# Attention outputs kept in DRAM until the merge, three more projections by seven products, and the merge's pools one block earlier

## The chip, the cores and the metric

The kernel runs on one core of a Trainium2 chip. The metric is the device time of one execution in microseconds (us). TensorE (PE) multiplies matrices, VectorE (DVE) and ScalarE (ACT) do elementwise work, GpSimd (POOL) and SyncE (SP) mostly issue transfers.

## The reference, cut to what matters

One decoder layer on 256 tokens of width 2048, in fp32, with 256 memory tokens:

```python
h = rmsnorm(x, attn_norm)
gq, gk, gv, gr, ga1, sq, sk, sv, mq, gates = split(h @ w_in)
log_a = log_sigmoid(ga1 @ gla_w_a2 + gla_b_a) / 16
o_gla = rmsnorm(gla_mixer(gq, gk, gv, log_a))              # 4 heads, d_k 128, d_v 256
y_gla = (o_gla * silu(gr)) @ w_br_gla
y_sb  = stick_breaking_mixer(rmsnorm(sq), rmsnorm(sk), sv) @ w_br_sb     # 8 heads of 128
m_k, m_v = split(rmsnorm(mem, mem_norm) @ w_mem_kv)
y_mem = memory_mixer(rmsnorm(mq), rmsnorm(m_k), m_v) @ w_br_mem          # 4 heads of 256
g = sigmoid(gates)
x = x + (g[0] * y_gla + g[1] * y_sb + g[2] * y_mem) @ w_o
gate, up = split(rmsnorm(x, ffn_norm) @ w_gate_up)          # width 5632 each
x = x + (silu(gate) * up) @ w_down
```

## The kernel before

Every product of fp32 matrices is made of three matmuls on rounded halves: high by high, high by low, low by high. The activations lie transposed as such pairs (`xTh`/`xTl`; `oh`/`ol` for attention outputs). Weights come from DRAM in tiles of 1 MB (`raw`, four k-tiles of 128x512), loaded by SP into slots of the list `free_raw`. Each half of a raw tile is split when it is needed: ACT casts it to the high part (`wh`, L137), DVE subtracts to get the low part (`wl`, L138). The two go into a split pair, which `parts()` takes in turn from the pools in `splits`. A pair feeds 128x512 matmuls into accumulators (`acc`, `tmp`) in PSUM.

`gemm` makes one block of 512 output columns, 12 matmuls for a pair (L209 to L211). `sgemm` makes two blocks at once. Over the first `2p` k-tiles it uses seven products instead of eight (`p1` to `p7`, L248 to L251, 6 matmuls for a pair), and over the rest plain products (`rest`, 12 for a pair). Its weight operands are sums of raw tiles, made by DVE (L263) or by POOL's accumulating loads (L305, L325); its activation operands (`forms`: `sh`, `sl`) are made once by `make_forms`. `put` sends a finished product on: a copy on ACT (L288) into an accumulator or a spare tile, or a subtraction on DVE (L290). `p5` is copied to a spare (L319). `result` adds the spare to the accumulator (L380). The list `seq` sets the order of products and rests.

Side work (norms with `normed_T`, attention, transposes) is written as generators in `background`; `step()` runs one piece after each pair, `flush()` runs what is left. A scheduler then sets each engine's order; an engine works in its order, and a wait holds up all that stands behind it.

The order of the program: `mems` and the memory projections `mk` and `mv` (about 100 us), evacuated from PSUM by ACT (L473); `mq` by `gemm`; `sq`, `sk`, `sv_` by `sgemm` with memory attention and norms beside them; `gqk` and `gv` by `gemm` with stick-breaking attention beside them; the decay projection `w_ga` (L762 to L764); `gr` by `gemm`, with the linear attention `gla()` begun behind its first block; four blocks of the first gate (`O_G`) with `w_br_mem`, merged by DVE (L936); release of the attention pools, making of `ring2` and `mrg`; two passes of `w_gate` by `sgemm` with `w_br_sb` and `w_br_gla`; `w_o`; the feed-forward network in three parts.

Pools share room. `opool` holds the pairs of the memory tokens, then of the outputs `o_mem` and `o_sb`, then of `o_gla`. The sigmoid of `gr` and of the first gate takes three ACT operations and one on DVE (L775 to L778), and `gr` is scaled at L907. Transposes are at L431 and their scaled split at L140 and L141.

Of the kernel before, what the change touches and what calls it, by code (L numbers as in the profile page):

```python
# [77 lines left out]
def trunk(ctx: ExitStack, tc: tile.TileContext, a, out):  # L78
# [137 lines left out]
    def sgemm(xs, forms, w, blks, p, row0=0, late=False, moved=False):  # L216
# [517 lines left out]
    def s_out(h):  # L734
# [34 lines left out]
    def sigmoid(dst, o, t, table):  # L769


        if table:
            act.activation(dst, o, AF.Sigmoid, scale=r_x[:, t : t + 1])
        else:
            act.activation(dst, o, AF.Exp, scale=nr_x[:, t : t + 1])  # L775
            dve.tensor_scalar(dst, dst, 3e38, None, op0=ALU.min)
            act.activation(dst, dst, AF.Ln, bias=1.0)
            act.activation(dst, dst, AF.Exp, scale=-1.0)  # L778
# [8 lines left out]
    gr = section("gr", "b")  # L787

    def gla():
        for t in range(2):  # L790
# [55 lines left out]
            og = opool.tile([P, GH, GDV], F32, name="g_og", tag="g_og")  # L846
# [276 lines left out]
```

## Time and profile before

| what | value |
|---|---|
| median of three runs | 1645.92 us (1645.72 to 1649.11) |
| profiled execution, its own time | 1647.21 us |
| its span in the trace | 1645.4 us |
| mean granted clock of TensorE | 0.999 |
| read from HBM, written to it | 320.89 MB, 8.39 MB |

The span runs from the first to the last instruction; an execution's own time has a little more around it. "Granted clock" is the share of TensorE's full speed that it was given; 1.00 is full speed.

### The profile page before, as it was taken

To read this page: it belongs to the slowest core of one execution; us is meant where nothing else is said; L and a number is where in the kernel's file an instruction comes from. 1 tells how busy PE (TensorE), PEld (TensorE's weight loads), DVE (VectorE), ACT (ScalarE), POOL (GpSimd) and SP (SyncE) were. 2 spreads that over 40 slices of the span, in tenths; PEclk is the share of its full clock that TensorE was granted. 3 is DMA by queue.
4 is the path that set the end of the run, shared out by engine and by line. 5 is a ranking of instruction groups with operands and counts; after the bars stand their busy time and mean duration, and the time that the engine had idled before them with its cause. 6 is when DMAs were issued, how large, how long until landed. Compare 5 with 4: busy or idle time off the path is not lost.

```text
span 1645.4 us, 19330 instructions
## 1 busy us (share of the span) xinstructions
PE 1629.8 (99%) x7314; PEld 1334.9 (81%) x7314; DVE 1291.2 (78%) x1491; ACT 988.0 (60%) x1204; POOL 53.8 (3%) x70
## 2 busy tenths in 40 slices
PE   8999999999999999999999999999999999999998
PEld 6888787888877878888888888888888888888887
DVE  6857788764565667887897798988888998888994
ACT  7755666654644556556555666666666666666662
POOL 0000000000000000000000000000110000110000
PEclk9999999999999999999999999999999999999999
DMA  8784575544544467667556758686897686897692
GB/s 327 280 325 125 189 249 158 200 161 156 183 154 154 157 228 284 191 215 255 174 210 220 254 181 259 216 298 234 258 274 255 193 302 240 257 271 253 193 343 89
DMA packets 59406, 368.82 MB, mean 224 GB/s; under 512 B 6544, under 2 KB 11152, under 8 KB 16688
## 3 DMA queue, kind: packets, MB, share of 16 engines
q1 hardware_dynamic: 49968, 320.17, 53.4%
q0 software_dynamic: 8704, 46.67, 14.2%
q8 instruction: 57, 0.93, 0.2%
q10 hardware_dynamic: 640, 0.75, 0.1%
q14 instruction: 37, 0.30, 0.1%
HBM read 320.89 MB, written 8.39 MB: 200 GB/s over the span
## 4 chain that ended last, share of the span: by engine, by line
PE 96%; DVE 1%; DMA 1%; ACT 1%; issue 0%; ACTq 0%; DVEq 0%
PE acc L250 15%; PE acc L251 15%; PE acc L248 15%; PE acc L209 10%; PE acc L210 10%; PE acc L211 10%; PE tmp L250 5%; PE tmp L251 5%; PE tmp L248 5%; PE tmp L431 2%; DVE wl L138 1%; ACT wh L137 1%; DMA raw<-in_w_gate_up 1%; DMA raw<-in_w_mem_kv 0%; PE tmp L635 0%; PE tmp L863 0%
## 5 line engine op out<-in xcount | busy, mean ns | idle before, releaser
L138 DVE TENSOR_TENSOR wl<-raw,wh 128x1024 fp32r<-128x1024 f32 (+1 forms) x728 | 876.9, 1220 | 278.4 <-ACT wh L137 267.4
L137 ACT CAST wh<-raw 128x1024 fp32r<-128x1024 f32 (+1 forms) x728 | 753.9, 1051 | 536.1 <-PE acc L211 212.9
L251 PE MATMUL acc<-wh,hl 128*128 128x512 f32 x452 | 175.9, 389 | 0.0
L250 PE MATMUL acc<-wl,hh 128*128 128x512 f32 x452 | 175.9, 389 | 0.0
L248 PE MATMUL acc<-wh,hh 128*128 128x512 f32 x452 | 175.8, 390 | 0.0
L209 PE MATMUL acc<-wh,xTh 128*128 128x512 f32 x384 | 152.7, 398 | 0.0
L211 PE MATMUL acc<-wh,xTl 128*128 128x512 f32 x384 | 149.9, 390 | 0.0
L210 PE MATMUL acc<-wl,xTh 128*128 128x512 f32 x384 | 149.8, 390 | 0.0
L263 DVE TENSOR_TENSOR raw<-raw 128x1024 f32<-128x1024 f32 x115 | 139.7, 1221 | 4.5 <-DMA raw<-in_w_gate_up 3.0
L209 PE MATMUL acc<-wh,oh 128*128 128x512 f32 x320 | 125.2, 393 | 2.6 <-ACT wh L137 1.6
L210 PE MATMUL acc<-wl,oh 128*128 128x512 f32 x320 | 124.9, 390 | 1.1 <-DVE wl L138 1.1
L211 PE MATMUL acc<-wh,ol 128*128 128x512 f32 x320 | 124.8, 390 | 0.0
L248 PE MATMUL acc<-wh,xTh 128*128 128x512 f32 x280 | 110.1, 395 | 1.3 <-ACT wh L137 1.3
L250 PE MATMUL acc<-wl,xTh 128*128 128x512 f32 x280 | 109.7, 392 | 0.5 <-DVE wl L138 0.5
L251 PE MATMUL acc<-wh,xTl 128*128 128x512 f32 x280 | 109.4, 391 | 0.0
L250 PEld LDWEIGHTS acc<-wl,hh 128*128 128x128 f32 x452 | 84.9, 188 | 17.7
L248 PEld LDWEIGHTS acc<-wh,hh 128*128 128x128 f32 x452 | 84.7, 188 | 17.8 <-ACT wh L137 0.2
L251 PEld LDWEIGHTS acc<-wh,hl 128*128 128x128 f32 x452 | 84.8, 188 | 17.6
L248 PE MATMUL tmp<-wh,sh 128*128 128x512 f32 x222 | 89.4, 403 | 1.8 <-ACT wh L137 1.7
L250 PE MATMUL tmp<-wl,sh 128*128 128x512 f32 x222 | 87.3, 393 | 0.7 <-DVE wl L138 0.7
L251 PE MATMUL tmp<-wh,sl 128*128 128x512 f32 x222 | 87.6, 395 | 0.0
L209 PEld LDWEIGHTS acc<-wh,xTh 128*128 128x128 f32 x384 | 72.2, 188 | 16.4 <-issue 2.2
(297 smaller groups left out, 2497.1 us busy)
## 6 DMA issues: line engine op xcount, KB each, us to landing
raw<-in_w_gate_up SPq DMA_DIRECT2D x88, 1024.0 KB, 5.9
raw<-in_w_in SPq DMA_DIRECT2D x72, 1024.0 KB, 4.9
raw<-in_w_down SPq DMA_DIRECT2D x44, 1024.0 KB, 6.5
raw<-raw POOLq DMA_DIRECT2D x35, 1024.0 KB, 7.9
raw<-in_w_gate SPq DMA_DIRECT2D x32, 1024.0 KB, 4.9
raw<-in_w_o SPq DMA_DIRECT2D x16, 1024.0 KB, 5.0
raw<-in_w_mem_kv SPq DMA_DIRECT2D x15, 1024.0 KB, 5.4
raw<-in_w_br_mem SPq DMA_DIRECT2D x8, 1024.0 KB, 5.2
```

Source lines behind the costliest of these rows:

```text
L137: act.copy(hi, src)
L138: dve.tensor_tensor(lo, src, hi.bitcast(F32), op=ALU.subtract)
L209: pe.matmul(o[t][:], xh[:, s], wh[:, j], start=k == 0, stop=False)
L210: pe.matmul(o[t][:], xh[:, s], wl[:, j], start=False, stop=False)
L211: pe.matmul(o[t][:], xl[:, s], wh[:, j], start=False, stop=k == nk - 1)
L248: pe.matmul(dst[:], xh, wh, start=id(dst) not in begun, stop=False, skip_group_check=True)
L250: pe.matmul(dst[:], xh, wl, start=False, stop=False, skip_group_check=True)
L251: pe.matmul(dst[:], xl, wh, start=False, stop=last, skip_group_check=True)
L263: dve.tensor_tensor(x, x, y, op=ALU.add)
L431: pe.transpose(dst, src, ident)
```

## The change

Memory attention's and stick-breaking attention's outputs no longer stay in SBUF as split pairs. `put_out` copies each piece (ACT, L639) and writes it to DRAM (`od_mem`, `od_sb`); `fetch_out` loads each back with one transfer of 1 MB behind `gr` and splits it there. In the room that `opool` held until then lies `ring_a`, two raw slots and two split pairs; the memory tokens' pairs lie in the same room before it, in a pool `mems`. `gqk`, `gv` go through `sgemm` with `p` = 2 and `gr` with `p` = 4, and `gr` stands ahead of `w_ga`. `ring2` and `mrg` are made ahead of the last `O_G` block. `seq` has one form for all calls that are not `late`, and the POOL sum in `p2` becomes the default (`w_down` keeps DVE's).

```diff
             prod(o[0, 0], single(0, 0), 11, last)
-            if moved:
+            if moved and not late:
                 nc.gpsimd.dma_start(q[11][0][:, :p], q[21][0][:, :p], accum_op=ALU.add)
...
         def q4(last):
-            prod(o[1, 0], single(0, 1), 11, last, *([] if moved else [(11, 21)]))
+            prod(o[1, 0], single(0, 1), 11, last, *([] if moved and not late else [(11, 21)]))
         def p5():
...
             seq = [a, *l21, b, *l11, *r0, *r1[:1], (made,), g, *l22, *r1[1:2], h, e, *l12, *r1[2:3], i, f, *r1[3:]]
-        elif moved:
-            seq = [a, g, *r0[:2], h, *r0[2:], b, e, *r1[:2], i, *r1[2:3], f, *r1[3:]]
-        elif p == SP:
-            seq = [a, g, *r0[:2], h, *r0[2:], e, *r1[:2], i, b, *r1[2:3], f, *r1[3:]]
         else:
-            seq = [a, *l21, g, *r0[:2], h, *r0[2:], e, *l12, *r1[:1], i, *l22, b, *l11, *r1[1:3], f, *r1[3:]]
+            seq = [a, *l21, *r0[:2], g, *r0[2:], h, *l22, b, *l11, e, *l12, *r1[:2], i, *r1[2:3], f, *r1[3:]]
         uses = {21: [a, g, h, f, *l21], 22: [g, h, i, *l22], 11: [b, f, *l11], 12: [h, e, *l12]}
...
     g_gla = gain["gla_out_norm"]
-    opool = tc.alloc_tile_pool(name="opool", bufs=2)
+    opool = tc.alloc_tile_pool(name="mems", bufs=2, side="right", reuse_waits="tile")
     sec = tc.alloc_tile_pool(name="sec", bufs=1)
...
     def outT():
-        return [opool.tile([P, 8, T], F32R, tag=f"o{x}", name=f"o{x}") for x in "hl"]
+        return [opool.tile([P, 8, T], F32R, tag="o", name=f"o{x}", bufs=4) for x in "hl"]
     mems = load_T([outT(), outT()], a["memT"], g_mem, mempool)
...
     att = tc.alloc_tile_pool(name="att", bufs=2)
-    pre = tc.alloc_tile_pool(name="pre", bufs=1, reuse_waits="tile")
-    free_raw.extend([(pre, "raw", 1), (opool, "oh", 2), (opool, "ol", 2)])
+    pre = widen("pre", 1, 0, "left")
+    opool.release()
+    ring_a = widen("ring_a", 2, 2)
     def ring(tag, bufs, dtype=F32):
...
         return ring("rd", 2, F32R)
-    o_mem = outT()
+    def outside(name):
+        return dram.tile([P, 8, T], F32, name=name)
+    def put_out(o, c, src):
+        n = src.shape[1] // T
+        v = rb()[:, : n * T]
+        act.copy(v, src)
+        nc.scalar.dma_start(o[:, c : c + n], v.rearrange("p (c t) -> p c t", c=n))
+    def fetch_out(o):
+        high, low = outT()
+        def work():
+            raw, done = loads()
+            v = raw[:].rearrange("p g n -> p (g n)").rearrange("p (c t) -> p c t", c=8)
+            nc.sync.dma_start(v, o[:])
+            yield
+            for c in range(0, 8, 4):
+                split(high[:, c : c + 4], low[:, c : c + 4], v[:, c : c + 4])
+                if c == 4:
+                    done()
+                yield
+        background.append(work())
+        return high, low
+    od_mem, od_sb = outside("od_mem"), outside("od_sb")
     m_pr, m_prT = {}, {}
...
                 )
-        split(*(x[:, 2 * h : 2 * h + 2].rearrange("p c t -> p (c t)") for x in o_mem), o[:])
-    def wide(dst, c0):
-        for j, result in sgemm(xs, sx, w_in, (c0 // NB, c0 // NB + 1), SP, moved=True):
+        put_out(od_mem, 2 * h, o[:])
+    def wide(dst, c0, p=SP):
+        for j, result in sgemm(xs, sx, w_in, (c0 // NB, c0 // NB + 1), p):
             for t in range(2):
...
-    o_sb = outT()
+    def sigmoid(dst, o, t, table):
+        if table:
+            act.activation(dst, o, AF.Sigmoid, scale=r_x[:, t : t + 1])
...
         pe.matmul(o[:, P:T], sv_[:, 1, h * SD : (h + 1) * SD], ls[:, T:W], start=False, stop=True)
-        split(o_sb[0][:, h], o_sb[1][:, h], o[:, :T])
+        put_out(od_sb, h, o[:, :T])
     flush()
...
     gqk, gv = section("gqk", "a"), section("gv", "d")
-    project(gqk, xs, w_in, O_GQ, r_x)
-    project(gv, xs, w_in, O_GV, r_x)
-    free_raw[:] = [x for x in free_raw if x[0] is not pre]
-    pre.release()
+    wide(gqk, O_GQ, 2)
+    wide(gv, O_GV, 2)
+    flush()
+    sqT = None
+    gr = section("gr", "b")
+    for j, result in sgemm(xs, sx, w_in, (O_GR // NB, O_GR // NB + 1), SP):
+        for t in range(2):
+            sg, o = ra()[:], result(t)
+            sigmoid(sg, o, t, False)
+            v = gr[:, t, j * NB : (j + 1) * NB]
+            act.activation(v, o, AF.Copy, scale=r_x[:, t : t + 1])
+            dve.tensor_tensor(v, v, sg, op=ALU.mult)
+    narrow(ring_a)
+    opool = tc.alloc_tile_pool(name="opool", bufs=4, side="right", reuse_waits="tile")
+    o_mem, o_sb = fetch_out(od_mem), fetch_out(od_sb)
+    narrow(pre)
     gl = tc.alloc_tile_pool(name="gl", bufs=1, reuse_waits="tile")
...
                     yield
-    for n in range(0, MIX, NB):
-        o = gemm(xs, w_in, O_GR + n)
-        if n == 0:
-            background.append(gla())
-        for t in range(2):
-            sg = gate()
-            sigmoid(sg, o[t][:], t, False)
-            v = gr[:, t, n : n + NB]
-            act.activation(v, o[t][:], AF.Copy, scale=r_x[:, t : t + 1])
-            dve.tensor_tensor(v, v, sg, op=ALU.mult)
+    background.append(gla())
     def to_chunks(src, n, hi, lo, gain):
...
     for n in range(0, D, NB):
+        if n + NB == D:
+            flush()
+            gl.release()
+            att.release()
+            sec.release()
+            ring2 = widen("ring2", 3, 1, "left")
+            kit = mrg = tc.alloc_tile_pool(name="mrg", bufs=1, reuse_waits="tile")
         g = gemm(xs, w_in, O_G + n)
...
         merge(sg, gemm(xo, a["w_br_mem"], n), n, True)
-    flush()
-    gl.release()
-    att.release()
-    sec.release()
-    widen("ring2", 3, 1)
-    kit = mrg = tc.alloc_tile_pool(name="mrg", bufs=1, reuse_waits="tile")
     background.append(gla_T())
...
             blks = (n0 // NB, n0 // NB + 1)
-            for j, result in sgemm(fs, sd, a["w_down"], blks, 4, row0=4 * part[0]):
+            for j, result in sgemm(fs, sd, a["w_down"], blks, 4, row0=4 * part[0], moved=False):
                 n = n0 + j * NB
...
```

The three places below show orders of instructions with the numbers of the tiles; nothing in them is a time. In the changed kernel most lines have moved by 4 to 8 and more: L145 and L146 are the cast and the subtraction of `split` (before: L137, L138), L271 is DVE's sum (L263), L298 and L384 the subtraction in `put` and the addition in `result` (L290, L380), L477 the evacuation of `mk`, `mv`, `mq` (L473), L736 to L739 the sigmoid (L775 to L778), L796 the scaling of `gr` (L907), L913 the square in `gla` (L872).

**First place: DVE at the start of the call for `sv_`.** `raw_2112` (before) and `raw_2123` (after) are its first raw tile, L487 is the norm of `sk`. Before:

```order
L263 TENSOR_TENSOR raw_2112<-raw_2112,raw_2148 128x1024
L380 TENSOR_TENSOR two_2043<-acc_1735,two_2043 128x512
L138 TENSOR_TENSOR wl_2132<-raw_2112,wh_2131 128x1024
L138 TENSOR_TENSOR wl_2152<-raw_2112,wh_2151 128x1024
L380 TENSOR_TENSOR two_2043<-acc_1736,two_2043 128x512
L487 TENSOR_REDUCE hn_ss_2124<-ra_2128 128x4
L487 TENSOR_REDUCE hn_ss_2124<-ra_2141 128x4
L263 TENSOR_TENSOR raw_2112<-raw_2112,raw_2148 128x1024
L487 TENSOR_REDUCE hn_ss_2124<-ra_2144 128x4
L263 TENSOR_TENSOR raw_2112<-raw_2112,raw_2242 128x1024
L146 TENSOR_SCALAR rs_m_2161<-hn_ss_2124 128x16
L138 TENSOR_TENSOR wl_2190<-raw_2112,wh_2189 128x1024
```

Of the change:

```order
L146 TENSOR_TENSOR wl_2126<-raw_2123,wh_2125 128x1024
L298 TENSOR_TENSOR two_2054<-two_1656,tmp_1748 128x512
L271 TENSOR_TENSOR raw_2123<-raw_2123,raw_2221 128x1024
L146 TENSOR_TENSOR wl_2143<-raw_2123,wh_2142 128x1024
L146 TENSOR_TENSOR wl_2162<-raw_2159,wh_2161 128x1024
L271 TENSOR_TENSOR raw_2123<-raw_2123,raw_2221 128x1024
L384 TENSOR_TENSOR two_2054<-acc_1746,two_2054 128x512
L146 TENSOR_TENSOR wl_2205<-raw_2159,wh_2204 128x1024
L146 TENSOR_TENSOR wl_2225<-raw_2123,wh_2224 128x1024
```

Ahead of the second L271 sum there are now the subtractions of `wl_2143` and `wl_2162`, the latter for the first rest, and the reductions of the norm no longer stand between the two sums.

**Second place: ACT from `gr` over `w_ga` to the first `O_G` block.** Before, `w_ga` (`wh_3275`, `wh_3303`) stands behind `gv`, and the first block of `gr` (`wh_3342`) follows:

```order
L137 CAST wh_3234<-raw_3232 128x1024
L137 CAST wh_3250<-raw_3232 128x1024
L137 CAST wh_3275<-raw_3272 128x1024
L137 CAST wh_3303<-raw_3272 128x1024
L137 CAST wh_3342<-raw_3340 128x1024
L473 ACTIVATE gv_2483<-acc_3128,r_x_114 128x512
L473 ACTIVATE gv_2483<-acc_3129,r_x_114 128x512
L137 CAST wh_3358<-raw_3340 128x1024
```

Of the change, where `wh_3674` and `wh_3702` are `w_ga`'s, `oh_3663` and `oh_3665` the fetched outputs, `two_3572` a finished product of `gr`, and `wh_3753` the first of `O_G`:

```order
L145 CAST wh_3674<-raw_3671 128x1024
L296 COPY two_3572<-tmp_3331 128x512
L145 CAST wh_3702<-raw_3671 128x1024
L145 CAST oh_3663<-raw_3732 128x1024 x2
L145 CAST oh_3665<-raw_3738 128x1024 x2
L736 ACTIVATE ra_3620<-two_3572,nr_x_118 128x512
L796 ACTIVATE gr_3326<-two_3572,r_x_117 128x512
L736 ACTIVATE ra_3644<-acc_3328,nr_x_118 128x512
L738 ACTIVATE ra_3620<-ra_3620 128x512
L796 ACTIVATE gr_3326<-acc_3328,r_x_117 128x512
L739 ACTIVATE ra_3620<-ra_3620 128x512
L738 ACTIVATE ra_3644<-ra_3644 128x512
```

Four casts of fetched outputs and the sigmoids of `gr` now stand between `w_ga`'s casts and the first cast of `O_G`.

**Third place: ACT at the start of the last `O_G` block.** Before, this is the end of the last block, where `wh_4763` is `w_br_mem`'s last and `wh_4815` the first of `w_gate`:

```order
L775 ACTIVATE sg_4699<-acc_4561,nr_x_115 128x512
L777 ACTIVATE sg_4699<-sg_4699 128x512
L775 ACTIVATE sg_4700<-acc_4562,nr_x_115 128x512
L778 ACTIVATE sg_4699<-sg_4699 128x512
L137 CAST wh_4763<-raw_4745 128x1024
L777 ACTIVATE sg_4700<-sg_4700 128x512
L137 CAST wh_4815<-raw_4796 128x1024
L778 ACTIVATE sg_4700<-sg_4700 128x512
L137 CAST wh_4798<-raw_4796 128x1024
```

Of the change, where `wh_4649` is `w_br_mem`'s last of the third block, `wh_4680` and `wh_4696` the first two of the last block, and `wh_4680` lies in `ring2`:

```order
L736 ACTIVATE sg_4584<-acc_4364,nr_x_118 128x512
L145 CAST wh_4649<-raw_4631 128x1024
L738 ACTIVATE sg_4584<-sg_4584 128x512
L145 CAST wh_4696<-raw_4678 128x1024
L739 ACTIVATE sg_4584<-sg_4584 128x512
L145 CAST wh_4714<-raw_4712 128x1024
L145 CAST wh_4730<-raw_4712 128x1024
L145 CAST wh_4748<-raw_4746 128x1024
L145 CAST wh_4680<-raw_4678 128x1024
L145 CAST wh_4764<-raw_4746 128x1024
```

The half that the block uses first is now cast behind four others of the block, `wh_4748` the last of them.

## Rows read from the trace of the kernel before

**Rows 1.** The page's first part: busy time, share of the span and instructions of each engine.

```profile
PE 1629.8 (99%) x7314; PEld 1334.9 (81%) x7314; DVE 1291.2 (78%) x1491; ACT 988.0 (60%) x1204; POOL 53.8 (3%) x70
```

**Rows 2.** Windows: PE, PEld, DVE, ACT, POOL busy (x starts), clock, DMA share, GB/s.

```profile
178.00:182.00 4.00, 2.60 (x11) 1.54 (x10) 2.41 (x5) 3.98 (x8) 0.00 (x0) 1.00 0.00 0
249.00:257.00 8.00, 6.36 (x20) 4.27 (x19) 8.00 (x14) 5.39 (x7) 0.85 (x1) 0.79 0.68 131
...
604.00:615.00 11.00, 8.38 (x38) 5.78 (x37) 9.54 (x13) 7.38 (x11) 0.86 (x1) 1.00 0.82 263
```

**Rows 3.** PE's timeline at place A; start, duration, what, idle before it.

```profile
179.57 0.73 PE L248 MATMUL acc<-wh,xTh 128*128 128x512 f32 x2 [0.87 <-ACT wh L137]
180.84 0.50 PE L250 MATMUL acc<-wl,xTh 128*128 128x512 f32 x1 [0.53 <-DVE wl L138]
```

**Rows 4.** PE's timeline at place B, the start of the call for `sv_`.

```profile
251.45 0.50 PE L248 MATMUL tmp<-wh,sh 128*128 128x512 f32 x1 [1.01 <-ACT wh L137]
252.39 0.73 PE L248 MATMUL acc<-wh,xTh 128*128 128x512 f32 x2 [0.45 <-ACT wh L137]
253.31 0.80 PE L250 MATMUL tmp<-wl,sh 128*128 128x512 f32 x1 [0.18 <-DVE wl L138]
```

**Rows 5.** DVE's timeline at place B.

```profile
249.10 1.22 DVE L263 TENSOR_TENSOR raw<-raw 128x1024 f32<-128x1024 f32 x1
...
252.03 1.22 DVE L138 TENSOR_TENSOR wl<-raw,wh 128x1024 fp32r<-128x1024 f32 x1
```

**Rows 6.** PE's and ACT's timelines at place C.

```profile
606.79 0.50 PE L250 MATMUL tmp<-wl,xTh 128*128 128x512 f32 x1 [1.32 <-DVE wl L138]
...
609.19 0.39 PE L251 MATMUL tmp<-wh,xTl 128*128 128x512 f32 x1
610.30 0.50 PE L248 MATMUL tmp<-wh,sh 128*128 128x512 f32 x1 [0.73 <-ACT wh L137]
...
611.76 0.50 PE L250 MATMUL tmp<-wl,sh 128*128 128x512 f32 x1 [0.51 <-DVE wl L138]
...
605.29 0.84 ACT L140 ACTIVATE oh<-tmp,vecs 128x256 fp32r<-128x256 f32 x2 [5.76 <-PE tmp L431]
608.25 2.00 ACT L137 CAST wh<-raw 128x1024 fp32r<-128x1024 f32 x2 [2.13 <-PE tmp L251]
```

**Rows 7.** ACT's timeline from the end of `mv` into `mq`.

```profile
98.74 0.69 ACT L473 ACTIVATE mv_mqT<-acc,r_mem 128x512 f32<-128x512 f32 x1 [0.57 <-PE acc L211]
99.33 1.04 ACT L137 CAST wh<-raw 128x1024 fp32r<-128x1024 f32 x1
101.46 1.05 ACT L137 CAST wh<-raw 128x1024 fp32r<-128x1024 f32 x1 [1.09 <-PE acc L211]
104.18 1.05 ACT L137 CAST wh<-raw 128x1024 fp32r<-128x1024 f32 x1 [1.67 <-PE acc L211]
```

**Rows 8.** Groups of ACT and DVE: count, busy us, mean ns, idle before.

```profile
L137 ACT CAST wh<-raw 128x1024 fp32r<-128x1024 f32 x726 | 752.7, 1052 | 534.9 <-PE acc L211 212.9 <-PE acc L251 197.0 <-DVE raw L263 52.4
...
L288 ACT COPY acc<-tmp 128x512 f32<-128x512 f32 x23 | 13.2, 572 | 16.0 <-PE tmp L251 15.7
...
L138 DVE TENSOR_TENSOR wl<-raw,wh 128x1024 fp32r<-128x1024 f32 x726 | 875.5, 1222 | 278.4 <-ACT wh L137 267.4
```

**Rows 9.** ACT's timeline behind the second block of `gr`.

```profile
422.42 0.69 ACT L775 ACTIVATE sg<-acc,nr_x 128x512 f32<-128x512 f32 x1 [0.31 <-PE acc L211]
...
426.45 1.04 ACT L137 CAST wh<-raw 128x1024 fp32r<-128x1024 f32 x1
```

**Rows 10.** PE's timeline in `w_ga`, its first two of 48 matmuls.

```profile
396.04 0.28 PE L762 MATMUL tmp<-xTh,wh 128*128 128x256 f32 x1
396.15 0.28 PE L763 MATMUL tmp<-xTl,wh 128*128 128x256 f32 x1
```

**Rows 11.** DMA issues: count, KB each, us from issue to landing.

```profile
raw<-in_w_in SPq DMA_DIRECT2D x72, 1024.0 KB, 4.9
...
raw<-raw POOLq DMA_DIRECT2D x35, 1024.0 KB, 7.9
```

More of the change, by code (lines that the diff above doesn't have):

```diff
@@ L88, in trunk, with widen, narrow @@
     free_raw, splits, turn = [], [], [0]
-    def widen(name, raw, w):
-        pool = ctx.enter_context(tc.tile_pool(name=name, bufs=1, side="right", reuse_waits="tile"))
-        free_raw.extend([(pool, "raw", raw)] * raw)
+    def widen(name, raw, w, side="right"):
+        pool = tc.alloc_tile_pool(name=name, bufs=1, side=side, reuse_waits="tile")
+        free_raw.extend([(pool, raw)] * raw)
         splits.extend([(pool, w)] * w)
-    pad = ctx.enter_context(tc.tile_pool(name="pad", bufs=1, side="right"))
+        return pool
+    def narrow(pool):
+        for x in (free_raw, splits):
+            x[:] = [y for y in x if y[0] is not pool]
+        pool.release()
+    pad = tc.alloc_tile_pool(name="pad", bufs=1, side="right")
     pad.tile([P, PAD], F32, name="pad")
-    widen("ring1", 3, 4)
+    ring1 = widen("ring1", 3, 4)
+    gog = tc.alloc_tile_pool(name="gog", bufs=2, side="right")
     small = ctx.enter_context(tc.tile_pool(name="small", bufs=2))
@@ L161, in loads @@
     def loads():
-        slot = pool, tag, bufs = free_raw.pop(0)
-        return pool.tile([P, KG, NB], F32, tag=tag, name="raw", bufs=bufs), lambda: free_raw.append(slot)
+        slot = pool, bufs = free_raw.pop(0)
+        return pool.tile([P, KG, NB], F32, tag="raw", name="raw", bufs=bufs), lambda: free_raw.append(slot)
     def parts():
@@ L178, in piece @@
         if not halves:
-            two = opool.tile([P, 2, NB], F32, name="two", tag="g_og")
+            two = gog.tile([P, 2, NB], F32, name="two", tag="g_og")
             halves.extend([two[:, 1], two[:, 0]])
@@ L214, in gemm, with sgemm @@
         return o
-    def sgemm(xs, forms, w, blks, p, row0=0, late=False, moved=False):
+    def sgemm(xs, forms, w, blks, p, row0=0, late=False, moved=True):
         nk = len(xs)
@@ L695, in trunk @@
     wide(sv_, O_SV)
-    free_raw[:] = [x for x in free_raw if x[0] is not opool]
-    o_sb = outT()
+    def sigmoid(dst, o, t, table):
+        if table:
+            act.activation(dst, o, AF.Sigmoid, scale=r_x[:, t : t + 1])
+        else:
+            act.activation(dst, o, AF.Exp, scale=nr_x[:, t : t + 1])
+            dve.tensor_scalar(dst, dst, 3e38, None, op0=ALU.min)
+            act.activation(dst, dst, AF.Ln, bias=1.0)
+            act.activation(dst, dst, AF.Exp, scale=-1.0)
     W = 3 * P
@@ L767, in trunk @@
     flush()
[L769 to L778, printed above, removed]
     def gate():
-        return gl.tile([P, NB], F32, tag="sg", name="sg", bufs=2)[:]
+        return piece()[:] if kit is not None else gl.tile([P, NB], F32, tag="sg", name="sg", bufs=2)[:]
     S = [gl.tile([P, GDV], F32, name=f"S{h}", bufs=1) for h in range(GH)]
@@ L845, in gla @@
             yield
[L846 removed]
+            og = gog.tile([P, GH, GDV], F32, name="g_og", tag="g_og")
             ss = small.tile([P, GH], F32, name="g_ss")
@@ L1018, in trunk @@
     opool.release()
-    kit = ctx.enter_context(tc.tile_pool(name="ffn", bufs=1, reuse_waits="tile"))
-    widen("ring3", 0, 1)
+    gog.release()
+    ring3 = widen("ring3", 0, 1)
+    kit = ffn = tc.alloc_tile_pool(name="ffn", bufs=1, reuse_waits="tile")
     sf = make_forms([(hh, hl)], form_tiles())
@@ L1028, in trunk @@
         for i in part:
-            for j, result in sgemm(hs, sf, a["w_gate_up"], (i, NF + i), 4 if i else 2, late=i == 0, moved=i > 0):
+            for j, result in sgemm(hs, sf, a["w_gate_up"], (i, NF + i), 4 if i else 2, late=i == 0):
                 if j == 0:
@@ L1075, in trunk @@
                     nc.gpsimd.dma_start(x2d[:, t, n : n + NB], v[:], accum_op=ALU.add)
+    for pool in (ffn, ring3, ring2, ring1, pad):
+        pool.release()
 def kernel(**inputs):
```

3 lines of the change are left out of this document (1 added, 2 removed).

## Prediction

> **What bounds the kernel now.** The first view to read is the page's table of engines: PE is busy for 1629.8 of 1645.4 us, DVE for 78% and ACT for 60% [rows 1]. So the time is TensorE's matmuls, one behind the other, plus the few places where PE stands still. The second view gives the price of a matmul. Where nothing is in the way, ACT's casts of a plain `gemm` follow each other at 101.46 and 104.18 us, each let go by PE [rows 7]: 2.72 us for the 12 matmuls of one split pair, 0.2267 us for a matmul of 128x512. The third view, PE's own timeline with its waits, shows where PE stands still for more than half a microsecond in the part that the change touches. There are three places.
>
> Place A, memory attention beside the first seven-product call: PE waits 0.87 us for a cast and 0.53 us for a subtraction [rows 3]. Each such wait costs some 0.16 us more than its idle time, since a matmul's 0.39 us normally overlaps the next one's start 0.23 us later. A costs 1.4 + 0.3 = 1.7 us.
>
> Place B, the start of the call for `sv_`: window 249:257 holds 20 matmul starts, which take 20 x 0.2267 = 4.5 us elsewhere, so 3.5 us are lost [rows 2]. DVE is busy for the whole window: `p5`'s sums (L263) from 249.10, the norm's reductions (L487) between them, and the subtraction that PE needs only at 252.03 [rows 5], while PE waits three times [rows 4]. The granted clock of the window is 0.79. The clock has two levels, 1.2 and 2.4 GHz, so 2 x 0.21 x 8 = 3.4 us of it were at the lower one, and half of that, 1.7 us, belongs to the 3.5.
>
> Place C, the first `w_gate` call behind the release of the attention pools: waits of 1.32, 0.73 and 0.51 us, while ACT stood 5.76 us with a transposed linear attention chunk (L140) at the head of its queue [rows 6]. That is 2.56 + 0.5 = 3.0 us.
>
> **What the change removes.** Matmuls first. Two column blocks over `2p` k-tiles take 24p matmuls plain (two blocks, two token halves, three matmuls each) and 7 x 3p = 21p by seven products. `gqk` and `gv` with `p` = 2 save 6 each, `gr` with `p` = 4 saves 12. Together 24 x 0.2267 = 5.4 us, all on PE.
>
> A, B and C go in the new order. At a call's start the rests `r0[:2]` now stand ahead of `p5`, so the two sums on DVE have two whole pairs of plain matmuls (5.4 us) of cover, which was not there at B; through this stretch there are also two more split pairs, in `ring_a`, so casts run further ahead at A. At C the last weight buffers and the merge's pool are made a block earlier, and the transposes of `gla_T` stand one by one between pairs. I take all three as gone, 1.7 + 3.5 + 3.0 = 8.2 us; the low bound is 5.5, with A's first wait and half of C left, since the softmax's exponentials and the casts of `gla_T` remain. Removed in all: 13.6 us (10.9 at least).
>
> **What it adds on the engines beside PE.** The 12 more splits are a cast of 1.05 us on ACT and a subtraction of 1.22 us on DVE each [rows 8]; the attention outputs' 12 small splits become 12 ACT copies and DMA issues, with four casts and four subtractions of 128x1024 when they are fetched. Over the whole span ACT has 40% and DVE 22% free, so in general this hides behind PE. Where DVE is fullest, in the calls for `gqk` and `gv`, a product pair gives it 1.36 us for 1.22 us of subtraction beside the stick-breaking work; I put 0.4 us there (0 to 1.5). POOL's accumulating loads rise from 38 to 49. One takes 7.9 us to land [rows 11] and in a call over eight k-tiles three plain pairs and four of products, 13.6 us of matmuls, stand between such a sum and its use, so it costs nothing; if one were late, PE would wait for the difference.
>
> The copy of `p1`'s result into `acc` (L288) used to have `p5`'s 6 or 12 matmuls behind it. Now the rests accumulate onto it, and in ten calls only 3 or 4 matmuls stand between. The last matmul of `p1` takes 0.39 us (at 609.19 [rows 6]) and the copy 0.57 [rows 8], 0.96 us until the copy is done, against 4 x 0.2267 = 0.91 until the first matmul that wants it: 0.05 us each, 0.5 us in all. A cast in ACT's way would add up to 1.05 us. Against that speaks that ACT was idle 16.0 us before these 23 copies, 15.7 of them for PE [rows 8]: it stands ready.
>
> **New waits.** A pool laid over another's room waits for that room's last reader, and on ACT and DVE everything later in the queue waits with it. The orders show three places.
>
> F, about 99 us: the first split pair of `mq` lies in `ring_a`, the room of the memory tiles, so the pair can't be written before the last matmul of `mv`; ACT's cast stands behind the two evacuations of `mv` as well. In the kernel before, the evacuation after that matmul starts at 98.74 and the cast behind it ends at 100.37, 1.63 us later [rows 7], with PE already fed from other pairs. Now PE waits for this, then for the subtraction (1.22 us), less two matmuls that run between (0.45), plus 0.16: 2.5 us.
>
> E, about 550 us: the same at the last `O_G` block, shown above. The cast `wh_4748`, which waits for the previous block's last matmul, stands ahead of `wh_4680`, which PE needs first: two casts (2.0 us as at 608.25 [rows 6]), the subtraction 1.22, less 0.45, plus 0.16: 2.9 us.
>
> G, about 425 us, from `gr` over `w_ga` to `O_G`: ACT has four casts of fetched outputs and eleven sigmoid and copy operations ahead of `wh_3753`. The first cast waits for a pair whose last matmul lies 18 matmuls (4.1 us) ahead of `w_ga`. Four casts of 1.05 end 0.1 us behind `w_ga`'s start. Eleven operations at the step of [rows 9] (seven in 4.03 us, 0.58 each) take 6.3, the next cast 1.05: 7.5 us. PE has 48 matmuls 0.11 us apart [rows 10], 5.4 us, and one more small one, about 0.3. So PE waits 1.8 us, and 0.5 more for what is left of the subtraction: 2.3 us (1.2 to 5; the upper end if the fetch of `od_sb`, priced like a weight load of 4.9 us [rows 11], comes late).
>
> Between them F, G and E cost 7.7 us. From below: F and E at the first cast alone, 1.6 and 1.0, and G nothing, 2.6 us.
>
> **The sum.** -5.4 - 8.2 + 7.7 + 0.4 + 0.5 = -5.0 us. Of the three places before, A and C kept the clock at 1.00 and B fell to 0.79 [rows 2]. After F or E one such fall would give back 1.7 us. Between none and one I take 0.8: -4.2 us. The profiled execution took 1647.21 us for a span of 1645.4, 1.3 above the median of 1645.92, which is one of three values from 1645.72 to 1649.11; differences carry over to the median: 1645.9 - 4.2 = 1641.7 us.
>
> **A rule on the clock.** Row first: PE idled three times at B and the clock fell to 0.79; at A and C it idled as long in all and kept 1.00 [rows 2 to 4, 6]. The Trainium skill (TensorE: Matmul & The Clock Gate, What's actually happening) says that "the default state is throttled, and activity releases the throttle", so that a wait of PE is paid a second time at the lower clock. B agrees with it, A and C do not show it.
>
> **The rivals.** (1) Forecast: F, G and E as priced, no more than one clock fall, 1639 to 1644 us. Chance 0.43. (2) The new waits are partly covered, near their lower bounds: -13.6 + 2.6 + 0.9 = -10 us, 1634 to 1639. For it: an order is no time, and where ACT and DVE run further ahead than I count, part of a wait is over before PE comes to it. Against: the order on PE has no other matmul to run between. Chance 0.2. (3) Every new wait is followed by matmuls at the lower clock, as behind B: 3 x 1.7 = 5.1 on -5.0, so 1646 us, no change that can be told. This is the case that the rule of the Trainium skill above would make. The same end comes if A and C stay and G takes 5. For it: F and E idle PE longer at a stretch than A or C do. Chance 0.25. (4) Slower: the copy under `p1` is what PE waits for. 26 calls have it now ahead of rests; at 0.36 us each it costs 9.4 instead of 0.5, 1650.6 us. It decides from (4.2 + 3.3) / 26 = 0.29 us more per call on. For it: 3 to 10 matmuls of cover against 12 to 20 before in most; against it: ACT waiting for PE at these copies. Chance 0.12.
>
> **How the numbers follow.** About 0.2%, 3.3 us, is what a measurement of this kernel can tell from no change. Case 2 and three quarters of case 1 lie more than that below, 0.2 + 0.32; with the lower end of case 3, 0.02, this makes 0.54 faster. The upper end of case 3, 0.03, and case 4 make 0.15 slower. What is left, 0.11 of case 1 and 0.2 of case 3, is 0.31 for no change. The range runs from case 2's middle to within case 4's threshold, 1635 to 1649 us; the forecast's own is 1639 to 1644.
>
> **What the changed profile would show.** PE x7290 instead of x7314 with some 24 fewer 128x512 matmuls; no PE wait over 0.5 us at the places of A, B, C; new PE waits for a cast and then a subtraction at the first pair of `mq`, behind `w_ga`, and at the start of the last `O_G` block, and granted clocks below 1.00 in these windows where case 3 holds. Case 4 would show as PE waiting for L288's copy (its line after is L296) at the start of most calls. The prediction is wrong if these waits are absent, or if a wait sits where I found cover: in the feed-forward calls, or at POOL's sums.

## The result, and the profile after

The changed kernel took 1655.79 us (median of five runs, 1653.70 to 1658.93) against 1647.20 us for the kernel before on the same chip (five runs, 1645.72 to 1649.11): ratio 1.0054, 95% interval 1.0037 to 1.0070. It is 0.5% slower, where the forecast was 1641.7 us and faster, with 1635 to 1649 us as its range.

The page's table of engines, to be held against [rows 1]:

```profile
PE 1633.6 (99%) x7290; PEld 1333.5 (81%) x7290; DVE 1308.4 (79%) x1506; ACT 1012.6 (61%) x1229; POOL 62.9 (4%) x81
```

The 24 matmuls are gone (x7290), and PE is "busy" 3.8 us longer all the same: its matmuls are longer. The page's chain shows where else the span went. First the kernel before, then the change:

```profile
PE 96%; DVE 1%; DMA 1%; ACT 1%; issue 0%; ACTq 0%; DVEq 0%
PE 87%; DVE 3%; ACT 2%; DMA 1%; issue 1%; DVEq 0%; ACTq 0%
```

PE's timeline at the places F, G and E of the prediction (about 99, 450 and 579 us), each row with the idle time before it:

```profile
98.86 0.39 PE L219 MATMUL acc<-wh,ol 128*128 128x512 f32 x1
101.34 0.73 PE L217 MATMUL acc<-wh,xTh 128*128 128x512 f32 x2 [2.09 <-ACT wh L145]
102.60 0.50 PE L218 MATMUL acc<-wl,xTh 128*128 128x512 f32 x1 [0.52 <-DVE wl L146]
...
450.52 1.12 PE L837 MATMUL tmp<-rb,gaT 16*128 16x512 f32 x2 [0.51 <-DVE gaT L820]
451.57 0.73 PE L217 MATMUL acc<-wh,xTh 128*128 128x512 f32 x2
452.58 0.78 PE L218 MATMUL acc<-wl,xTh 128*128 128x512 f32 x1 [0.28 <-DVE wl L146]
...
579.03 0.39 PE L219 MATMUL acc<-wh,ol 128*128 128x512 f32 x1
581.50 0.73 PE L217 MATMUL acc<-wh,xTh 128*128 128x512 f32 x2 [2.08 <-ACT wh L145]
583.10 0.80 PE L218 MATMUL acc<-wl,xTh 128*128 128x512 f32 x1 [0.87 <-DVE wl L146]
583.69 0.63 PE L219 MATMUL acc<-wh,xTl 128*128 128x512 f32 x1
584.12 0.63 PE L217 MATMUL acc<-wh,xTh 128*128 128x512 f32 x1
```

F and E show the two waits that were forecast, for a cast and then for a subtraction. At G no wait for a cast shows. The chain there runs through ACT as forecast, from the casts of the fetched outputs (`oh`) to the late cast of `wh`:

```profile
441.18 2.95 ACT oh L145 x3
...
450.33 0.94 ACT wh L145
...
451.30 1.24 DVE wl L146
...
452.58 0.78 PE acc L218
```

But PE has something else to do until the cast is done: it waits 0.51 us for `gaT`, DVE's copy of `w_ga`'s result, and runs the linear attention's first two matmuls (L837) until 451.57. Only the subtraction is waited for, 0.28 us.

I price a place by PE's start-to-start distances, as far as they exceed the 0.2267 us of an undisturbed matmul. F is 3.2 us. Behind G and E the matmuls also last 0.63 instead of 0.39 us and start 0.43 us apart: TensorE ran at its lower clock. E costs 6.2 us with that, 2.9 of them for the clock. G costs 3.4, of which 0.8 are L837's matmuls and stood in the kernel before as well; of the 2.6 left, 1.7 are the clock.

Two places were not foreseen. The first holds PE's longest wait on another engine, 4.47 us. ACT's timeline and then PE's, in the call for `sk`; "ACTq" is ACT issuing a transfer:

```profile
198.22 0.59 ACT L639 COPY rb<-tmp 128x512 f32<-128x512 f32 x1
198.84 0.33 ACTq L640 DMA_DIRECT2D od_mem<-rb  x1
...
202.15 0.72 ACT L709 ACTIVATE sq<-two,r_x 128x512 f32<-128x512 f32 x1
208.02 0.58 ACT L639 COPY rb<-tmp 128x512 f32<-128x512 f32 x1 [5.15 <-DMA od_mem<-rb]
...
213.81 0.57 ACT L296 COPY acc<-tmp 128x512 f32<-128x512 f32 x1
```

```profile
209.57 0.39 PE L258 MATMUL acc<-wl,xTh 128*128 128x512 f32 x1
214.44 0.80 PE L256 MATMUL acc<-wh,xTh 128*128 128x512 f32 x1 [4.47 <-ACT acc L296]
```

Read it backwards. PE waits for the copy under `p1` (L296). That copy stands at the end of a queue on ACT whose first, the last head's `put_out` (L639 at 208.02), waited 5.15 us for its tile `rb`. There are two `rb` tiles. Each is taken by `m_turn` or `put_out` in turn, and one that `put_out` used comes free only when its write to DRAM has landed. The chain names the transfer:

```profile
198.84 9.11 DMA od_mem<-rb
```

The second place is the same thing with stick-breaking attention's writes. DVE's timeline, and PE's:

```profile
337.74 0.56 DVE L760 SCALAR_TENSOR_TENSOR rb<-tmp,ra 128x384 f32<-128x384 f32 x1 [1.97 <-DMA od_sb<-rb]
```

```profile
338.69 0.70 PE L779 MATMUL tmp<-ra,skT_sv 128*128 128x256 f32 x2 [1.57 <-DVE ra L774]
```

The windows of the first place, of E and of G, and then those of A, B and C, now without idle time; columns as in [rows 2]:

```profile
207.00:222.00 15.00, 10.53 (x35) 8.07 (x34) 9.68 (x16) 8.90 (x12) 0.00 (x0) 0.77 0.30 110
576.00:592.00 16.00, 13.05 (x45) 9.92 (x44) 9.23 (x14) 4.84 (x5) 0.00 (x0) 0.79 0.74 297
444.00:458.00 14.00, 13.22 (x71) 10.71 (x70) 11.96 (x17) 11.86 (x19) 0.00 (x0) 0.88 0.68 236
...
178.00:182.00 4.00, 4.00 (x20) 3.13 (x19) 2.01 (x4) 1.99 (x3) 0.00 (x0) 1.00 0.57 217
249.00:257.00 8.00, 8.00 (x37) 6.64 (x36) 8.00 (x9) 5.91 (x9) 0.86 (x1) 1.00 0.46 154
592.00:615.00 23.00, 23.00 (x103) 19.07 (x102) 12.81 (x12) 11.99 (x15) 0.00 (x0) 1.00 0.60 223
```

Window 207:222 has 35 matmul starts where some 66 would fit. The place costs 7.6 us, and 1.7 us more are lost at 337.

A sum by places, against the kernel before, each over its whole stretch and so only roughly: matmuls -5.4; A -1.2, B -3.1, C -2.8; F +3.2, G +2.6, E +6.2; the writes +7.6 and +1.7; small waits in the calls for `gqk` and `gv` about +2. Together about +11; the spans differ by 10.3 us, the medians by 8.6.

### The profile page after: what moved, and what is told of

Same layout as the page of the kernel before. It is cut to its first block, busy times and chain, and to the rows that moved or that the text cites. A ratio compares the mean times of both kernels' runs of the same rounds, so it can differ in the third digit from the quotient of the medians.

```text
span 1655.7 us, 19396 instructions
## 1 busy us (share of the span) xinstructions
PE 1633.6 (99%) x7290; PEld 1333.5 (81%) x7290; DVE 1308.4 (79%) x1506; ACT 1012.6 (61%) x1229; POOL 62.9 (4%) x81
## 4 chain that ended last, share of the span: by engine, by line
PE 87%; DVE 3%; ACT 2%; DMA 1%; issue 1%; DVEq 0%; ACTq 0%
PE acc L256 17%; PE acc L259 17%; PE acc L258 16%; PE acc L218 6%; PE acc L219 6%; PE acc L217 6%; PE tmp L259 5%; PE tmp L256 5%; PE tmp L258 5%; PE tmp L435 2%; DVE wl L146 1%; ACT wh L145 1%; DMA od_mem<-rb 1%; PE tmp L904 0%; DMA od_sb<-rb 0%
## 5 line engine op out<-in xcount | busy, mean ns | idle before, releaser
L146 DVE TENSOR_TENSOR wl<-raw,wh 128x1024 fp32r<-128x1024 f32 (+1 forms) x740 | 891.7, 1219 | 274.2 <-ACT wh L145 261.4
L145 ACT CAST wh<-raw 128x1024 fp32r<-128x1024 f32 (+1 forms) x740 | 772.4, 1051 | 533.3 <-PE acc L259 247.1
L256 PE MATMUL acc<-wh,xTh 128*128 128x512 f32 x424 | 170.1, 401 | 4.8 <-ACT acc L296 4.8
L258 PE MATMUL acc<-wl,xTh 128*128 128x512 f32 x424 | 166.7, 393 | 0.0
L259 PE MATMUL acc<-wh,xTl 128*128 128x512 f32 x424 | 166.0, 394 | 0.0
L271 DVE TENSOR_TENSOR raw<-raw 128x1024 f32<-128x1024 f32 x114 | 138.2, 1218 | 0.8
L256 PEld LDWEIGHTS acc<-wh,xTh 128*128 128x128 f32 x424 | 80.3, 189 | 23.6 <-ACT acc L296 7.9
L259 PE MATMUL tmp<-wh,sl 128*128 128x512 f32 x246 | 96.0, 390 | 0.0
L258 PE MATMUL tmp<-wl,sh 128*128 128x512 f32 x246 | 95.8, 389 | 0.0
L259 PEld LDWEIGHTS acc<-wh,xTl 128*128 128x128 f32 x424 | 80.3, 189 | 17.0
L258 PEld LDWEIGHTS acc<-wl,xTh 128*128 128x128 f32 x424 | 80.4, 190 | 15.5
L217 PE MATMUL acc<-wh,xTh 128*128 128x512 f32 x192 | 76.7, 402 | 4.2 <-ACT wh L145 4.2
```

The costliest lines, as they stand in the source:

```text
L145: act.copy(hi, src)
L146: dve.tensor_tensor(lo, src, hi.bitcast(F32), op=ALU.subtract)
L217: pe.matmul(o[t][:], xh[:, s], wh[:, j], start=k == 0, stop=False)
L256: pe.matmul(dst[:], xh, wh, start=id(dst) not in begun, stop=False, skip_group_check=True)
L258: pe.matmul(dst[:], xh, wl, start=False, stop=False, skip_group_check=True)
L259: pe.matmul(dst[:], xl, wh, start=False, stop=last, skip_group_check=True)
```

## The experiments

Theory: each new wait is one of room, a tile or pool whose last reader or writer is late, passed on by ACT's or DVE's order, and each can be taken away by itself; the clock adds to it. Rivals: PE waits because the copy under `p1` lost its cover; or the engines are late in any case, and a wait removed comes back elsewhere. Ratios are to the kernel before, run beside each; where two kernels are compared, medians. The runs were spread over several chips, on which the median of the kernel before was between 1645.7 and 1647.2 us, so a difference of medians of 1.5 us or less shows nothing.

**Other tiles for the written outputs** (`e1_put`). `rc` and `rd` are free during memory attention, and `ls` has just been read by the product whose result is copied.

```diff
-    def put_out(o, c, src):
+    def put_out(o, c, src, place):
...
-        v = rb()[:, : n * T]
+        v = place[:, : n * T]
...
-        put_out(od_mem, 2 * h, o[:])
+        put_out(od_mem, 2 * h, o[:], (rc, rd)[h % 2]()[:].bitcast(F32))
...
-        put_out(od_sb, h, o[:, :T])
+        put_out(od_sb, h, o[:, :T], ls)
```

> Only the place where an attention output is copied before it is written to DRAM is changed: for memory attention the four tiles rc and rd, which nothing else uses in that stretch, for stick-breaking attention the tile ls that its product has just read, instead of the two rb tiles. First theory (the writes' landing holds the two rb tiles, ACT waits for it in order, and PE waits for ACT): the PE waits of 4.86 us at 209.6 and of 1.97 us at 336.7 go, with the matmuls at the lower clock behind the first (2.8 us together with it 7.6), so 1655.8 - 9.5 = about 1646 us. Rival (PE waits there because the copy under p1, L296, has too little cover): PE still waits for L296 at these places and the time stays within 2 us of 1655.8.

1645.49 us, ratio 0.9992 (0.9982 to 1.0001). Both waits are gone; the stretch of the first one is full, at clock 1.00:

```profile
200.00:220.00 20.00, 20.00 (x90) 16.62 (x89) 18.01 (x32) 14.93 (x20) 0.00 (x0) 1.00 0.62 178
```

The writes land no sooner (3.1 us in the middle, 2.9 in the change); only nobody waits for them. The thin cover stayed as it was, so the copy was only the messenger. Not all of the 10.3 us gained is the writes': in this trace less of the lower clock stands behind E, and none behind G, where PE waits as long as in the change:

```profile
436.00:452.00 16.00, 15.21 (x83) 12.38 (x82) 14.33 (x19) 14.34 (x22) 0.05 (x1) 1.00 0.78 270
```

**The turn of the split pairs** (`e2_turn`). `turn` is set so that `parts()` goes on with the first pair of `splits`, which lies in older room; the pairs of `ring_a` and of `ring2` come last.

```diff
     ring_a = widen("ring_a", 2, 2)
+    turn[0] = len(splits) - 1
...
             ring2 = widen("ring2", 3, 1, "left")
+            turn[0] = len(splits) - 1
```

> Only the turn of the split pairs is set, so that the first pairs of mq and of the last O_G block lie in ring1, whose room is free early, and the pairs of ring_a and ring2 come last in the turn. First theory (PE waits at F and E because the first pair lies in room that is still read): the waits of 2.48 and 0.92 us at 98.9 and of 2.47 and 1.26 us at 579 go, and the lower clock behind the second, 3.2 + 6.4 = 9.6 us, so about 1646 us. Rival (ACT is late there in any case, with evacuations and sigmoids): one half or less of it is gained, 1651 us or more.

1644.12 us, ratio 0.9990 (0.9980 to 0.9999): 11 us less than the change. PE's timeline shows no idle time at all at F or E. The first pair only had to lie in room that was already free. F and E were priced at 9.4 us; the other gain that the trace shows is at G, where one wait is left and the clock (440 to 455 us) is 1.00:

```profile
445.34 0.73 PE L217 MATMUL acc<-wh,xTh 128*128 128x512 f32 x2 [0.46 <-ACT wh L145]
```

**The fetch behind `w_ga`** (`e3_fetch`), with pauses between the load and its casts.

```diff
-            yield
+            for _ in range(4):
+                yield
...
-    o_mem, o_sb = fetch_out(od_mem), fetch_out(od_sb)
...
     dve.tensor_copy(gaT[:], p[:GR, :T])
     flush()
+    o_mem, o_sb = fetch_out(od_mem), fetch_out(od_sb)
```

> Only the fetching of the attention outputs is put behind w_ga, with pauses between its pieces; two of its four casts still stand ahead of the first cast of O_G in ACT's order, two come 20 rows later. First theory (the four casts ahead of O_G's first cast make the wait at 450): two casts less are 2.1 us, as much as the wait beyond w_ga, and the lower clock behind it (1.7 us) goes too, so about 1652.5 us. Rival (the eleven sigmoid and copy operations of gr alone are too much): the wait shrinks by less than 1 us, and the time stays at 1655 us.

1663.07 us, ratio 1.0100 (1.0085 to 1.0115): 7 us slower than the change, a miss of both theories. G shrinks, to 0.9 us. But `background` runs its pieces one after the other, so the linear attention behind the fetch begins later and its end is flushed at the start of the last `O_G` block, where E is. DVE's and PE's timelines there:

```profile
580.93 1.82 DVE L915 COPY g_og<-tmp 128x256 f32<-128x256 f32 x4 [1.03 <-ACT g_og L914]
...
586.89 1.22 DVE L921 TENSOR_TENSOR g_og<-g_og,gr 128x1024 f32<-128x1024 f32 x1
588.03 1.22 DVE L146 TENSOR_TENSOR wl<-raw,wh 128x1024 fp32r<-128x1024 f32 x1
```

```profile
583.28 1.16 PE L217 MATMUL acc<-wh,xTh 128*128 128x512 f32 x2 [2.46 <-ACT wh L145]
589.30 0.80 PE L218 MATMUL acc<-wl,xTh 128*128 128x512 f32 x1 [4.87 <-DVE wl L146]
```

**All three edits** (`e4_three`), and **without the late fetch** (`e8_two`).

> The edits of the three other kernels together. If the waits are separate, their gains add up: 9.5 + 9.6 + 3 = 22 us less, about 1634 us, below the kernel before. If they are not (a wait removed comes back at the next place where DVE or ACT is behind), less than two thirds of the sum: 1641 us or more.

1637.98 us, ratio 0.9950 (0.9935 to 0.9965).

> The changed kernel with two of the edits: other tiles for the written attention outputs, and the turn of the split pairs set at mq and at the last O_G block; the fetch stands where the change put it. First theory (these two waits are separate and the late fetch gained nothing): 1655.8 - 10 - 10.6 = about 1635 us, 0.7% under the kernel before. Rival (the waits are linked through ACT's and DVE's lateness): 1640 us or more.

1635.36 us, ratio 0.9936 (0.9924 to 0.9949). The gains of the first two edits, 10.3 and 11.7 us, add up to 22 of which 20.4 came; the lower clock behind G went in each of the two and can go only once. With the late fetch (`e4_three`) the kernel is no faster: 2.6 us slower by medians, but the two intervals overlap. `e8_two` beats the change and the kernel before, the latter by 0.64%. Its table of engines:

```profile
PE 1626.1 (100%) x7290; PEld 1330.0 (81%) x7290; DVE 1308.1 (80%) x1506; ACT 1013.6 (62%) x1229; POOL 63.0 (4%) x81
```

**Only `od_sb` fetched later** (`e11_fetch`): `e8_two`, and

```diff
-    o_mem, o_sb = fetch_out(od_mem), fetch_out(od_sb)
+    o_mem = fetch_out(od_mem)
...
     background.append(gla())
+    o_sb = fetch_out(od_sb)
```

> As the kernel with the two edits (1635.4 us), but od_sb is fetched behind the linear attention, so that two of the four casts leave the place behind w_ga while the linear attention begins no later. First theory (what is left of G there is 0.7 us): 0 to 1 us faster, 1634.5 to 1635.4. Rival (any cast of 1 MB put into the last O_G block makes PE wait, as the late fetch did): 2 us slower or more.

1635.07 us, ratio 0.9932 (0.9918 to 0.9946), not to be told from `e8_two`. The wait of 0.46 us that `e8_two` has left behind `w_ga` is gone, and PE does not wait in the last `O_G` block either.

**The order of products and rests.** `e5_oldseq` is `e8_two` with

```diff
-            seq = [a, *l21, *r0[:2], g, *r0[2:], h, *l22, b, *l11, e, *l12, *r1[:2], i, *r1[2:3], f, *r1[3:]]
+        elif p == SP:
+            seq = [a, g, *r0[:2], h, *r0[2:], b, e, *r1[:2], i, *r1[2:3], f, *r1[3:]]
+        else:
+            seq = [a, *l21, g, *r0[:2], h, *r0[2:], e, *l12, *r1[:1], i, *l22, b, *l11, *r1[1:3], f, *r1[3:]]
```

> The same two edits, and the order of products and rests inside a call as it was in the kernel before. First theory (the new order takes away the wait at the start of the call for sv_, 3.5 to 4 us, and at the start of w_gate, and its shorter cover for the copy under p1 costs some 0.05 us per call): 3 to 6 us slower than with the new order, 1638 to 1641 us. Rival (the copy under p1, L296, costs PE 0.2 us or more in each of 26 calls, so the old order is the better one): 2 us or more faster, 1633 us or less.

In `w_gate` and `w_down` this is not quite the old order: there `b` stood later before. 1635.20 us, ratio 0.9935 (0.9921 to 0.9948): no difference. B does not come back, and no gain from a longer cover shows. `b1_seq` is the kernel before with the new order alone:

> The kernel before, with nothing but the new order of products and rests. First theory: B's 3.5 us go, part of C, and at the copy under p1 26 x 0.05 = 1.3 us are added: 2 to 4 us faster than the kernel before, ratio 0.998 to 0.9988. Rival (the thin cover of the copy costs 0.2 us and more per call): 26 x 0.2 = 5.2 - 3.5, 2 us slower or more, ratio 1.001 or more.

1645.07 us, ratio 0.9996 (0.9987 to 1.0005): no change. A is gone (PE is busy throughout 174 to 184 us) and B is down to one wait of 0.85 us, but the copy is now waited for once at 147 and C is still there:

```profile
147.46 0.50 PE L248 MATMUL acc<-wh,xTh 128*128 128x512 f32 x1 [0.67 <-ACT acc L288]
...
251.10 0.50 PE L248 MATMUL tmp<-wh,sh 128*128 128x512 f32 x1 [0.85 <-ACT wh L137]
...
606.27 0.50 PE L250 MATMUL tmp<-wl,xTh 128*128 128x512 f32 x1 [1.75 <-DVE wl L138]
```

**Four pairs again** (`e9_fewer`): `e5_oldseq`, and

```diff
-    ring_a = widen("ring_a", 2, 2)
+    ring_a = widen("ring_a", 2, 0)
```

> As the kernel with the two edits and the old order of products, with one thing more: ring_a gives its two raw slots but no split pairs, so four pairs are left through the projections, as in the kernel before. First theory (the wait B of the kernel before went because casts and subtractions run two pairs further ahead, not because of the order of products): B comes back at the call for sv_ with 3 to 4 us, and A with 1 to 2, so 1639 to 1641 us. Rival (B went for another cause, such as the norms' place): within 1 us of 1635.3.

1644.71 us, ratio 0.9990 (0.9981 to 1.0000): 9.5 us slower than `e5_oldseq`, for two split pairs. PE's timeline at B, row by row the one of [rows 4], and at G:

```profile
250.40 0.50 PE L256 MATMUL tmp<-wh,sh 128*128 128x512 f32 x1 [1.00 <-ACT wh L145]
251.35 0.73 PE L256 MATMUL acc<-wh,xTh 128*128 128x512 f32 x2 [0.45 <-ACT wh L145]
252.26 0.50 PE L258 MATMUL tmp<-wl,sh 128*128 128x512 f32 x1 [0.18 <-DVE wl L146]
...
442.99 1.22 PE L217 MATMUL acc<-wh,xTh 128*128 128x512 f32 x2 [1.63 <-ACT wh L145]
444.71 0.80 PE L218 MATMUL acc<-wl,xTh 128*128 128x512 f32 x1 [0.50 <-DVE wl L146]
```

B is back with the same three waits, without a fall of the clock (2.5 us). G costs about 5 us more than in `e5_oldseq`, with the clock at 0.72 from 438 to 450 us; that was not expected. A was expected back and is not:

```profile
176.00:182.00 6.00, 6.00 (x29) 5.06 (x28) 3.13 (x4) 2.22 (x3) 0.00 (x0) 1.00 0.70 236
```

**The merge's pools.** `e6_ring2` is the changed kernel with `ring2` and `mrg` made behind the loop over `O_G`, as before; `e10_best` is the same with the edits of `e1_put` and of `e2_turn` at `mq`; `e13_c` is `e10_best` with the old order of products.

> The changed kernel with only ring2 and mrg made at the merge again, as in the kernel before. First theory (making them a block ahead costs the wait E, 6.1 us with the lower clock, and saves the wait C, 3 us): E goes, C comes back with at most 3 us, so 3 us faster than the changed kernel, about 1653 us. Rival (C was gone through the order of products alone): all of E's 6 us, about 1649.5 us. Second rival (the pools' order saves more than C): no faster, 1656 us.

1649.72 us, ratio 1.0023 (1.0013 to 1.0032), 6.1 us less than the change: PE is busy throughout 576 to 615 us, so E is gone and C is not back.

> The changed kernel with other tiles for the written outputs, the turn of the split pairs set at mq, and ring2 and mrg made at the merge as in the kernel before. First theory (the earlier pools bring nothing here, since the wait C does not come back without them): as fast as the kernel with the turn set at both places, 1635 us, within 1 us. Rival (with the other waits gone, C of 3 us comes back): 1638 us.

1636.97 us, ratio 0.9942 (0.9930 to 0.9955), its interval overlapping that of `e8_two`; no C.

> As the kernel with ring2 and mrg made at the merge again and the two other waits taken away (1637.0 us), but with the old order of products and rests. First theory (the wait C at the first w_gate call went for neither of the two alone, it needs both the late pools and the old order): C comes back with 2 to 3 us, 1639 to 1640 us. Rival (C went for a third cause: in the order on ACT, five casts of w_gate now stand ahead of the linear attention's pieces, where two did in the kernel before): no wait at the start of w_gate, within 1 us of 1637.

1637.18 us, ratio 0.9942 (0.9927 to 0.9957); no wait of PE at the start of `w_gate`. So C went neither through the earlier pools nor through the order of products. On ACT, three more casts of weights now stand ahead of the linear attention's pieces; why the scheduler placed them so stays open.

**Work for TensorE during E** (`e12_fill`): the changed kernel with matmuls whose result nothing reads.

```diff
+        if n + NB == D:
+            fill = tmp()
+            for _ in range(20):
+                pe.matmul(fill[:, :T], xs[0][0][:, :P], xs[0][0], start=True, stop=True)
         g = gemm(xs, w_in, O_G + n)
```

> The changed kernel with 20 matmuls of 128x256 on data at hand, whose result nothing reads, ahead of the last O_G block's first matmul: TensorE has work for 2.3 us of the wait E, nothing else moves. First theory (the clock falls there because TensorE stands still, and that is 2.8 us of E's 6.1): the granted clock stays at 1.00 in this stretch, and the time falls by 2 to 3 us, to about 1653 us. Rival (the wait is all and the clock adds nothing, or falls in any case): the same time as the changed kernel, 1655.8 us or more.

1653.01 us, ratio 1.0039 (1.0025 to 1.0053): 2.8 us less. PE's timeline and the window that had clock 0.79:

```profile
577.81 2.56 PE L989 MATMUL tmp<-xTh 128*128 128x256 f32 x20
580.21 0.63 PE L217 MATMUL acc<-wh,xTh 128*128 128x512 f32 x2
581.66 0.50 PE L218 MATMUL acc<-wl,xTh 128*128 128x512 f32 x1 [0.83 <-DVE wl L146]
```

```profile
576.00:592.00 16.00, 15.17 (x77) 12.64 (x75) 10.40 (x10) 5.51 (x6) 0.00 (x0) 1.00 0.77 310
```

PE is kept from its work as long as before (3.5 us); what went is the lower clock behind it, 2.9 us by start-to-start distances. The times alone do not show that much: the intervals of the two ratios overlap, and in this trace the lower clock behind G, which the edit does not touch, is missing too.

**Plain products for `gqk` and `gv`** (`e14_plain`): `e8_two` with `project` in place of `wide` there.

> As the kernel with the two edits (1635.4 us), with gqk and gv by plain products again, 12 matmuls of 128x512 more. First theory (these matmuls lie on TensorE with nothing else hidden or bared): 12 x 0.2267 = 2.7 us slower, 1638.1 us. Rival (DVE and the thin cover of the copy under p1 take the gain back in these two calls): within 1 us of 1635.4.

1637.05 us, ratio 0.9940 (0.9923 to 0.9957) against 0.9936: between the two, and not told apart from `e8_two`. In the traces, from ACT's last evacuation of a `sv_` accumulator to its first of a `gr` accumulator, it is 128.0 us in `e8_two` and 128.8 here. So of the 2.7 us that these 12 matmuls take, some 0.8 are gained, and about 1.9 go to small waits beside the products.

## Why the prediction was wrong

**The step that failed** is the one on what the change adds beside PE: "the attention outputs' 12 small splits become 12 ACT copies and DMA issues", which "in general" hides behind PE. It counted the engines' time (ACT 40% free) and not the tiles. A write to DRAM holds its source tile until it has landed (ACT waited 5.15 us for one at 208.02), and `put_out` had taken it from a ring of two that attention itself uses. That is 9.3 us at two places (`e1_put`), more than the whole forecast gain, and it was in no term, rival or bound. The work that was to hide it was never named.

**New waits.** F and E were at the right places, for the right reasons, as the rows after and `e2_turn` show. F was priced at 2.5 and measured 3.2 us. E was priced at 2.9 and measured 6.2: the wait itself is 3.3, and the rest is the clock. At G, priced at 2.3, ACT's queue was as late as forecast, but the "one more small one, about 0.3" on PE was a wait for `gaT` and L837's two matmuls, which filled the time until the cast was done. PE lost 0.9 us by waiting; that the place came to 2.6 is luck, since 1.7 of it are the clock. I allowed for no more than one fall; there were three, behind the writes, G and E. This part of rival 3 was right for this execution, and at E `e12_fill` takes the lower clock away by itself. The places behind the writes, G and E agree with the sentence quoted from the Trainium skill (TensorE: Matmul & The Clock Gate, What's actually happening), that "the default state is throttled, and activity releases the throttle". F, with 2.09 us of idle time and clock 1.00 in its window, does not, and neither does G in `e1_put`, with the waits of the change and clock 1.00.

**What the change removes.** The 24 matmuls are gone as forecast. A, B and C shrank by about 7.1 of the 8.2 us taken. For A the reason given was the two more split pairs, and the runs speak against it: A stays away with four pairs too, under the new order alone (`b1_seq`) and under the old one (`e9_fewer`). What takes it away there stays open. B's was given mainly as the order of products. That order alone does take most of B (`b1_seq`), but here it was not needed: with the old order and the pairs B stays away (`e5_oldseq`), with the old order and without them it returns (`e9_fewer`). C's reason, the earlier pools, is wrong (`e6_ring2`, `e13_c`): they bring no measurable gain and cost E.

**Rivals.** The one for slower, the copy under `p1`, came out on its side of the forecast and for another reason: PE waits for L296, but only because ACT was held (`e1_put`). Where ACT is free the thin cover costs nothing that can be measured (`e5_oldseq` against `e8_two`). The term for `gqk` and `gv`, 0.4 us with 1.5 as its bound, was too small; about 2 us of small waits stand there (`e14_plain`).

## What to carry to other kernels

When a result that stayed in fast memory is written out instead, count the tiles it is written from as well as the engine's time: each is held until the transfer has landed, and an engine that works in order passes that wait to all that queues behind it. When a pool is laid over another's room, the first instruction that uses it should be one that is wanted late; here one line at two places, which set the turn of the buffers, was worth 11 us. A wait of TensorE can cost nearly twice its length, as at E, and the bound of a forecast should hold the lower clock behind every new one.

## What the runs showed of the hardware that was not expected

A write of 256 KB to DRAM took 9.11 us to land where an accumulating transfer of POOL and a weight load of 1 MB each were under way; the twelve writes of the changed kernel took 1.9 to 9.1 us, 2.9 in the middle. No run shows whether those two transfers are the reason. The same waits were followed by the lower clock in one trace and not in another: B in the kernel before (0.79) and in `e9_fewer` (1.00), G in the change (0.88) and in `e1_put` (1.00).
